# One VectorE operation for the silu of the state-space convolution, tile by tile, and both decay increments made ahead

## The chip, the cores and the metric

The program runs on one core of a Trainium2 chip. The metric is the time of one execution on the device in microseconds (us). The kernel before took 2345.67 us, the median of three runs (2345.67, 2345.67 and 2346.8).

## The reference, cut to what matters

Two layers of a decoder trunk on 512 tokens of width 1024. In each layer one input projection of the normalised residual feeds four token mixers: A (dilated attention), B (retention), C (differential attention) and D (a Mamba-2 state space). Their outputs are gated, summed and projected; then come a cross-attention over 256 memory tokens and a SwiGLU. The change lies in D:

```python
xbc = conv(xbc, conv_w, 4 taps, depthwise, causal) + conv_b     # 1024 channels
xbc = silu(xbc)                                                 # a * sigmoid(a)
xs, Bm, Cm = split(xbc, (512, 256, 256))
dt = softplus(dt + dt_bias);  a_cum = cumsum(dt * A)            # 8 heads in 2 groups
Lmat = exp(where(causal, a_cum[i] - a_cum[j], -1e30))           # decay, per head and 128-token chunk
y_diag = einsum(C B^T * Lmat, x * dt);  y_off = C h_prev * exp(a_cum)
y = rmsnorm((y_diag + y_off + x * D) * silu(z))
```

## The kernel before, in words

All activations lie feature-major in tiles of 128 features by 512 tokens ("units", 59 of them; some in "quads" of four side by side). Each large product is made of three products in fp32r, high part by high, high by low and low by high (`mm3`, `tm`), so that PE gets 128x128 weights and 512 columns for each instruction.

**The weight stream.** The weights come in chunks of eight 128x128 blocks through SP's DMA queue (`load`, L231). `prep` makes of a chunk its high part on ACT (L245) and its low part on POOL or VectorE (L248; three chunks of five go to POOL). It is called when PE's program comes to a new chunk, and makes the chunk three places further on (`PREP = 3`); four buffers hold the high parts, four the low.

**The order of the work** is written out once, by a planner in Python; no engine reorders anything. PE's program is the large products of the projections. After every three products `beat` counts 3, and at each 6 (so every six products) `step` lets every active item of a queue go on by one stage. The items are generators: what they issue up to the next `yield n` goes into all engines' programs at this place, and they go on n steps later. At most three items are active, the others wait in order. `bu` waits for free units, `bgbanks` for PSUM banks, `turn` for a count that other items raise, `finish` makes steps without large products until the named items are done.

**State space.** The 1024 channels of x, B and C are eight tiles: the first four come out of one group of products at once, the other four one by one (`ev_rb`, L418). After every second tile an item `conv` is queued for the pair: bias and last tap on ACT (L705), six multiply-adds on VectorE (L708), after three steps the tanh on ACT (L713; all weights are halved, so silu(2a) = a tanh(a) + a), after two more a product (L716) and a sum (L718) for each tile on POOL. `dt_item` makes the step sizes and the increments of the decay. Then come the products for z (`tm`, 32 blocks), and after them `d_item` is queued for each of the four chunks of 128 tokens; it starts once all of `conv` and `dt_item` is done.

A `d_item` builds the decay as exp(products): `tri_a(g)` (L795, two POOL operations for a group of four heads, high and low part) writes the increments masked by a triangle into two units, PE multiplies them with the strict triangle `stri` (L825, L826, through L266), ACT takes the exponential (L827). Both groups use the same two units, so `tri_a(1)` is issued behind group 0's products, three steps before its own. Between lie the transposes of the chunk (L803), the copies out of PSUM (L810, L811, L812), the products with dt and the decay on VectorE (L818, L819) and the skip term on POOL (L820).

```python
tri_a(0)                                    # L800
... transposes, copies; yield 3; L818 to L820; yield 3
self.mm(self.P(b), self.stri, self.UR(ta[0]), True, False)   # L825, in the loop over g
if g == 0:
    tri_a(1)                                # L830
    yield 3
```

The queues behind this: ACT holds `prep`'s high parts and `conv`'s tanh in one program; POOL holds `prep`'s low parts, L716, L718, L795 and L820 in one program.

Of the kernel before, what the change touches and what calls it, by code (L numbers as in the profile page):

```python
# [12 lines left out]
AF = mybir.ActivationFunctionType  # L13
# [44 lines left out]
class Prog:  # L58
# [18 lines left out]

# [1 line left out]
    def unit(self, n=1, r=False):  # L79
        """n tiles of [128, 512]; r: for products, of 12 significant bits"""  # L80
        if self.nu < n:
            raise RuntimeError("out of units")
        self.nu -= n
        v = self.vid
        self.vid += n
        for i in range(v, v + n):
            self.tiles[i] = self.upool.tile([128, 512], F32R if r else F32, tag="u", name="u")
        return v

    def quad(self, r=False):  # L90
        """four tiles of [128, 512] side by side"""
        if self.nq < 1:
            raise RuntimeError("out of quads")
        self.nq -= 1
        v = self.vid
        self.vid += 4
        t = self.qpool.tile([128, 4, 512], F32R if r else F32, tag="q", name="q")
        self.quads[v] = t
        for i in range(4):
            self.tiles[v + i] = t[:, i]  # L100
        return v
# [44 lines left out]
    def bu(self, n=1, r=False):  # L146
        """units for background work, once enough are free"""
        while self.nu < n + self.reserve:
            yield
        us = [self.unit(r=r) for _ in range(n)]  # L150
        return us if n > 1 else us[0]
# [8 lines left out]

# [1 line left out]
    def add(self, name, gen):  # L162
# [7 lines left out]
    def turn(self, key, n):  # L170
        """waits for the n-th turn at key"""
        while self.turns.get(key, 0) < n:
            yield
# [12 lines left out]
    def go(self, it):  # L186
        """one stage of an item; it yields how many beats its next stage should wait"""
        it[2] -= 1
        if it[2] > 0:
            return  # L190
        try:
            it[2] = next(it[1]) or 1
        except StopIteration:
            self.active.remove(it)
            self.left[it[0]] -= 1
# [29 lines left out]

# [1 line left out]
    def load(self, n):  # L227
# [46 lines left out]
    def fm(self, name, l, cols, xs, evac, outer=False, k0=0, norm=None, need=None):  # L274
        """feature-major products: one bank per 128 columns; outer: all columns of one k before the next;
        norm: the outputs wait for the norm of the products' input, which is found meanwhile"""
        K = len(xs)
        if outer:
            bs = [self.bank() for _ in cols]
            for k in range(K):  # L280
                if need:
                    need(k)
                for j, c in enumerate(cols):
                    self.mm3(self.P(bs[j]), self.w(name, l, k0 + k, c), xs[k], k == 0, k == K - 1)

            def out():
                if norm:
                    self.norm_bcast()
                    norm()
                for j, b in enumerate(bs):  # L290
                    evac(j, self.P(b))
                    self.freebank(b)
            if norm:
                self.norm_stat()
                self.later = [18, out]
            else:
                out()
            return
        for j, c in enumerate(cols):
            b = self.bank()  # L300
            for k in range(K):
                self.mm3(self.P(b), self.w(name, l, k0 + k, c), xs[k], k == 0, k == K - 1)
            evac(j, self.P(b))
            self.freebank(b)

    def tm(self, name, l, c0, xs, evac, nt=NT):
        """token-major products: 512 columns, one bank per 128 tokens"""
        K = len(xs)
# [13 lines left out]

# [1 line left out]
    def rsqrt(self, v, w):  # L324
        """1/sqrt(v) of a [128, w] tile: bit guess and three Newton steps"""
        nc = self.nc
# [14 lines left out]
    def split(self, hi, lo, src):  # L341
        """hi + lo = src, each of 12 significant bits"""
        self.nc.scalar.activation(out=hi, in_=src, func=AF.Copy)  # L343
        self.nc.vector.tensor_tensor(out=lo, in0=src, in1=hi.bitcast(F32), op=OP.subtract)
# [9 lines left out]

# [1 line left out]
    def finish_x(self, d, ps, g, hi=True):  # L356
        """the residual tile d is final: its part of the norm and of the next input"""
        nc = self.nc
# [67 lines left out]

# [1 line left out]
    def a_item(self, pr, qb):  # L428
# [57 lines left out]

# [1 line left out]
    def c_item(self, h, qb):  # L488
# [84 lines left out]
    def tail(self, name, b, g, t):  # L573
        """a transposed bank [feature, 4, token] times its gains becomes a branch's input"""
        nc = self.nc
# [12 lines left out]

# [1 line left out]
    def b_item(self, l, t):  # L590
# [103 lines left out]

# [1 line left out]
    def conv(self, l, js):  # L696
        nc = self.nc
        cw = lambda i, j: self.cw[:, j * 4 + i:j * 4 + i + 1]
        X = [self.U(self.D[1] + j) for j in js]
        yield from self.turn("conv", js[0])  # L700
        us = yield from self.bu(2 * len(js))
        A = [self.U(u) for u in us[::2]]
        th = [self.U(u) for u in us[1::2]]
        for j, x, a in zip(js, X, A):
            nc.scalar.activation(out=a, in_=x, func=AF.Identity, scale=cw(3, j), bias=self.cw[:, 32 + j:33 + j])  # L705
        for i in range(1, 4):
            for j, x, a in zip(js, X, A):
                nc.vector.scalar_tensor_tensor(out=a[:, i:], in0=x[:, :T - i], scalar=cw(3 - i, j), in1=a[:, i:],  # L708
                                               op0=OP.mult, op1=OP.add)
        yield 3  # L710
        self.turns["conv"] = js[0] + 2
        for t, a in zip(th, A):
            nc.scalar.activation(out=t, in_=a, func=AF.Tanh)  # L713
        yield 2
        for x, t, a in zip(X, th, A):
            nc.gpsimd.tensor_tensor(out=x, in0=t, in1=a, op=OP.mult)  # L716
        for x, a in zip(X, A):
            nc.gpsimd.tensor_tensor(out=x, in0=x, in1=a, op=OP.add)  # L718
        for u in us:
            self.release(u)  # L720

# [59 lines left out]
    def d_item(self, l, c):  # L781
# [8 lines left out]
        b8 = lambda ap: ap.unsqueeze(2).to_broadcast([128, 8, 64])  # L790
        ta = yield from self.bu(2, True)

        def tri_a(g):
            for u, a in zip(ta, (S["ah"], S["al"])):
                nc.gpsimd.tensor_tensor(  # L795
# [3 lines left out]
                    op=OP.mult)  # L799
        tri_a(0)  # L800
        bs = yield from self.bgbanks(2)
        for j in range(4):
# [20 lines left out]
        for g in range(2):  # L823
            (b,) = yield from self.bgbanks(1)
            self.mm(self.P(b), self.stri, self.UR(ta[0]), True, False)  # L825
            self.mm(self.P(b), self.stri, self.UR(ta[1]), False, True)  # L826
            nc.scalar.activation(out=self.U(G[g]), in_=self.P(b), func=AF.Exp)  # L827
            self.bgfree(b)
            if g == 0:
                tri_a(1)  # L830
                yield 3
        yield 1
        self.release(ta[0])
        self.release(ta[1])
        for g in range(2):
# [71 lines left out]

# [1 line left out]
    def upgate(self, l, i, name):  # L909
# [43 lines left out]

# [1 line left out]
    def mem_load(self, i):  # L955
# [135 lines left out]

# [1 line left out]
    def ffn(self, l, g, last):  # L1093
# [51 lines left out]

# [1 line left out]
    def layer(self, l):  # L1147
# [41 lines left out]
        def ev_x(o):  # L1189
            f = self.ev_rb(xb + o)  # L1190

            def g(j, ps):
                f(j, ps)
                if j % 2:
                    self.add("Dc", self.conv(l, [o + j - 1, o + j]))
            return g
# [254 lines left out]
```

## Time and profile before

| | |
|---|---|
| profiled execution, span | 2340.9 us, 27338 instructions |
| the same kernel, timed runs | 2345.67, 2346.8, 2345.67 us |
| PE busy | 2285.5 us (98%) |
| VectorE (DVE) busy | 1170.2 us (50%) |
| ScalarE (ACT) busy | 820.9 us (35%) |
| GpSimd (POOL) busy | 656.2 us (28%) |
| mean granted TensorE clock | 0.993 |

The profiled execution has no time of its own beside its span; the timed runs lie 4.8 us above the span, which is what starts and ends an execution around its first and last instruction. "Busy" is the share of the span in which an engine executes; an arrow in a row names what an idle engine waited for; PEclk is the granted clock of TensorE, 1.00 for 2.4 GHz and 0.50 for 1.2 GHz.

### The profile page before, as it was taken

What the parts mean: (1) busy time and instruction counts of PE and PEld (TensorE: products, weight loads), DVE (VectorE), ACT (ScalarE), POOL (GpSimd) and SP (SyncE); (2) the same over time, 40 slices, a digit from 0 to 9 for tenths busy, and PEclk for the clock granted to TensorE, in tenths of its full rate; (3) what the DMA queues carried; (4) which work ended last, traced back from release to release, by engine and by line L of the source; (5) the groups of instructions that cost most, each with busy time, mean ns of one, the idle gap of its engine ahead of it and who ended that gap; (6) DMA issues with size and microseconds to landing.
All of it is one profiled execution on the core that took longest, in us unless ns stands there. A gap on an engine that the chain in (4) does not pass through costs nothing. (4 is left out here: it accounts for less than half of the span.)

```text
span 2340.9 us, 27338 instructions
## 1 busy us (share of the span) xinstructions
PE 2285.5 (98%) x10714; PEld 1835.9 (78%) x10714; DVE 1170.2 (50%) x2186; ACT 820.9 (35%) x1395; POOL 656.2 (28%) x327
## 2 busy tenths in 40 slices
PE   8999999999999999999999999999999999999997
PEld 6777777777888788888877777777878877888886
DVE  6755443545846554431347563355475655543321
ACT  5323433343234432222323244334423443322231
POOL 2463222213222122222237422222322222222221
PEclk9999999999999999999999999999999999999998
DMA  6122222223234223333322222222223432332331
GB/s 227 51 81 73 78 76 73 81 72 95 78 99 144 72 90 108 99 92 107 122 88 80 67 79 73 73 81 76 92 68 99 138 105 81 90 99 90 100 98 54
DMA packets 61473, 213.70 MB, mean 91 GB/s; under 512 B 7072, under 2 KB 7456, under 8 KB 61088
## 3 DMA queue, kind: packets, MB, share of 16 engines
q1 hardware_dynamic: 60624, 210.18, 28.7%
q8 instruction: 84, 1.38, 0.2%
q10 hardware_dynamic: 576, 1.05, 0.1%
q0 software_dynamic: 144, 0.73, 0.1%
q14 instruction: 45, 0.37, 0.0%
HBM read 207.73 MB, written 4.19 MB: 91 GB/s over the span
## 5 line engine op out<-in xcount | busy, mean ns | idle before, releaser
L266 PE MATMUL ps<-u,hi 128*128 128x512 f32 x4160 | 1301.9, 394 | 1.3 <-ACT u L343 0.7
L248 POOL TENSOR_TENSOR lo<-raw,hi 128x1024 fp32r<-128x1024 f32 x213 | 519.0, 2438 | 1567.8 <-ACT hi L245 1505.3
L266 PEld LDWEIGHTS ps<-u,hi 128*128 128x128 f32 x4160 | 772.6, 188 | 173.8 <-issue 12.9
L266 PE MATMUL ps<-u,lo 128*128 128x512 f32 x2080 | 812.3, 391 | 1.7 <-POOL lo L248 1.7
L245 ACT ACTIVATE hi<-raw 128x1024 fp32r<-128x1024 f32 x372 | 388.8, 1051 | 329.9 <-PE ps L266 220.1
L266 PEld LDWEIGHTS ps<-u,lo 128*128 128x128 f32 x2080 | 391.0, 188 | 85.3 <-POOL lo L248 2.4
L248 DVE TENSOR_TENSOR lo<-raw,hi 128x1024 fp32r<-128x1024 f32 x159 | 209.5, 1320 | 352.2 <-ACT hi L245 351.9
L266 PE MATMUL ps<-hi,u 128*128 128x512 f32 x896 | 289.9, 405 | 11.6 <-ACT hi L245 11.6
L266 PE MATMUL ps<-q,hi 128*128 128x512 f32 x768 | 240.8, 395 | 0.0
L266 PEld LDWEIGHTS ps<-hi,u 128*128 128x128 f32 x896 | 166.1, 192 | 56.0 <-ACT hi L245 12.9
L266 PE MATMUL ps<-lo,u 128*128 128x512 f32 x448 | 178.2, 398 | 6.7 <-POOL lo L248 5.6
L266 PE MATMUL ps<-u 128*64 128x128 f32 (+6 forms) x1208 | 171.0, 338 | 4.3 <-DVE u L418 2.1
L266 PEld LDWEIGHTS ps<-q,hi 128*128 128x128 f32 x768 | 141.3, 188 | 34.0 <-issue 5.2
L266 PEld LDWEIGHTS ps<-u 128*128 128x128 f32 (+2 forms) x1208 | 117.1, 172 | 47.5 <-issue 27.9
L266 PE MATMUL ps<-q,lo 128*128 128x512 f32 x384 | 149.8, 390 | 0.0
L921 ACT ACTIVATE u<-u 128x512 f32<-128x512 f32 x64 | 40.4, 631 | 210.9 <-DVE u L920 210.6
L266 PEld LDWEIGHTS ps<-lo,u 128*128 128x128 f32 x448 | 85.7, 191 | 28.3 <-POOL lo L248 6.9
L920 DVE TENSOR_TENSOR u<-ps,u 128x512 f32<-128x512 f32 x64 | 44.0, 688 | 121.8 <-PE ps L266 121.8
L266 PEld LDWEIGHTS ps<-q,lo 128*128 128x128 f32 x384 | 72.1, 188 | 15.5
L1108 DVE TENSOR_TENSOR u<-ps,u 128x512 f32<-128x512 f32 x44 | 30.4, 692 | 86.7 <-PE ps L266 85.9
L347 PE MATMUL ps<-gcst,u 128*128 128x128 f32 x416 | 65.9, 274 | 5.9 <-DVE u L684 2.8
L347 PEld LDWEIGHTS ps<-gcst,u 128*128 128x128 f32 x416 | 51.2, 140 | 23.0 <-DVE u L684 4.1
(209 smaller groups left out, 1657.2 us busy)
## 6 DMA issues: line engine op xcount, KB each, us to landing
raw<-wall SPq DMA_DIRECT2D x372, 512.0 KB, 3.5
q<-memt SPq DMA_DIRECT2D x6, 512.0 KB, 6.4
q<-xt SPq DMA_DIRECT2D x2, 1024.0 KB, 7.6
u<-rot SPq DMA_DIRECT2D x8, 256.0 KB, 4.1
u<-xt SPq DMA_DIRECT2D x8, 256.0 KB, 6.0
xd<-u SPq DMA_DIRECT2D x8, 256.0 KB, 2.0
u<-xd SPq DMA_DIRECT2D x8, 256.0 KB, 5.0
out<-u SPq DMA_DIRECT2D x4, 256.0 KB, 2.7
```

The costliest lines, as they stand in the source:

```text
L245: nc.scalar.activation(out=h, in_=r, func=AF.Copy)
L248: eng.tensor_tensor(out=lo, in0=r, in1=h.bitcast(F32), op=OP.subtract)
L266: self.nc.tensor.matmul(out, lhsT=a, rhs=b, start=start, stop=stop)
L347: self.nc.tensor.transpose(out, src, self.ident)
L920: nc.vector.tensor_tensor(out=self.U(u), in0=ps, in1=self.U(self.rb), op=OP.mult)
L921: nc.scalar.activation(out=self.U(u), in_=self.U(u), func=AF.Tanh, scale=0.5)
L1108: nc.vector.tensor_tensor(out=self.U(t), in0=ps, in1=self.U(self.rb), op=OP.mult)
```

## The change

`conv` becomes an item of one tile instead of two. It issues the bias and last tap on ACT, one step later three multiply-adds on VectorE, two steps later it lets the next tile's item begin, one step later the tanh on ACT, and two steps later one VectorE operation, x = (tanh + 1) * a, instead of the two on POOL. It is queued after every tile.

`d_item` takes four units for the increments instead of two. `tri_a(0)` stands where it stood, `tri_a(1)` two steps behind it and ahead of the transposes; the transposes and what follows them up to group 0's products move two steps back; the two groups' products are one step apart instead of three, and a group's units are released right behind its products. From `tri_a(0)` to the products with the decay (L837) it is ten steps as before. Comments are removed as well.

```diff
-    def conv(self, l, js):
+    def conv(self, l, j):
...
-        yield from self.turn("conv", js[0])
-        us = yield from self.bu(2 * len(js))
...
-        for j, x, a in zip(js, X, A):
-            nc.scalar.activation(out=a, in_=x, func=AF.Identity, scale=cw(3, j), bias=self.cw[:, 32 + j:33 + j])
+        yield from self.turn("conv", j)
+        ua, ut = yield from self.bu(2)
+        a, th = self.U(ua), self.U(ut)
+        nc.scalar.activation(out=a, in_=x, func=AF.Identity, scale=cw(3), bias=self.cw[:, 32 + j:33 + j])
+        yield 1
         for i in range(1, 4):
-            for j, x, a in zip(js, X, A):
-                nc.vector.scalar_tensor_tensor(out=a[:, i:], in0=x[:, :T - i], scalar=cw(3 - i, j), in1=a[:, i:],
-                                               op0=OP.mult, op1=OP.add)
-        yield 3
-        self.turns["conv"] = js[0] + 2
-        for t, a in zip(th, A):
-            nc.scalar.activation(out=t, in_=a, func=AF.Tanh)
+            nc.vector.scalar_tensor_tensor(out=a[:, i:], in0=x[:, :T - i], scalar=cw(3 - i), in1=a[:, i:],
+                                           op0=OP.mult, op1=OP.add)
         yield 2
-        for x, t, a in zip(X, th, A):
-            nc.gpsimd.tensor_tensor(out=x, in0=t, in1=a, op=OP.mult)
-        for x, a in zip(X, A):
-            nc.gpsimd.tensor_tensor(out=x, in0=x, in1=a, op=OP.add)
-        for u in us:
-            self.release(u)
+        self.passed("conv")
+        yield 1
+        nc.scalar.activation(out=th, in_=a, func=AF.Tanh)
+        yield 2
+        nc.vector.scalar_tensor_tensor(out=x, in0=th, scalar=1.0, in1=a, op0=OP.add, op1=OP.mult)
+        self.release(ua)
+        self.release(ut)
...
-        ta = yield from self.bu(2, True)
+        ta = yield from self.bu(4, True)
 
         def tri_a(g):
-            for u, a in zip(ta, (S["ah"], S["al"])):
+            for u, a in zip(ta[2 * g:2 * g + 2], (S["ah"], S["al"])):
...
         tri_a(0)
+        yield 2
+        tri_a(1)
         bs = yield from self.bgbanks(2)
...
-            self.mm(self.P(b), self.stri, self.UR(ta[0]), True, False)
-            self.mm(self.P(b), self.stri, self.UR(ta[1]), False, True)
+            self.mm(self.P(b), self.stri, self.UR(ta[2 * g]), True, False)
+            self.mm(self.P(b), self.stri, self.UR(ta[2 * g + 1]), False, True)
+            self.release(ta[2 * g])
+            self.release(ta[2 * g + 1])
             nc.scalar.activation(out=self.U(G[g]), in_=self.P(b), func=AF.Exp)
             self.bgfree(b)
-            if g == 0:
-                tri_a(1)
-                yield 3
-        yield 1
-        self.release(ta[0])
-        self.release(ta[1])
+            yield 1
...
-                if j % 2:
-                    self.add("Dc", self.conv(l, [o + j - 1, o + j]))
+                self.add("Dc", self.conv(l, o + j))
```

## Rows read from the trace of the kernel before

**Rows 1.** The page: span, and busy time and share of each engine.
```profile
span 2340.9 us, 27338 instructions
...
PE 2285.5 (98%) x10714; PEld 1835.9 (78%) x10714; DVE 1170.2 (50%) x2186; ACT 820.9 (35%) x1395; POOL 656.2 (28%) x327
```

**Rows 2.** Waits of PE, 60 to 220 us (layer 0): us in total, times, longest.
```profile
PE ps L266 <- POOL u L795: 7.1, 4, 3.8
PE ps L266 <- POOL lo L248: 3.4, 2, 1.7
...
PE ps L266 <- ACT hi L245: 0.3, 2, 0.2
```

**Rows 3.** Waits of PE, 1200 to 1300 us (layer 1), same columns.
```profile
PE ps L266 <- POOL lo L248: 3.9, 2, 2.2
PE ps L266 <- POOL u L795: 1.9, 3, 0.8
PE ps L266 <- ACT hi L245: 1.2, 1, 1.2
```

**Rows 4.** Busy time by stretch: window, us, engines' busy us (instructions), PEclk, DMA, GB/s.
```profile
70.00:112.00 42.00, 40.12 (x181) 32.56 (x180) 38.13 (x54) 12.68 (x19) 22.64 (x13) 1.00 0.18 56
116.00:120.00 4.00, 3.92 (x10) 3.16 (x11) 1.11 (x1) 2.48 (x5) 4.00 (x4) 0.57 0.38 131
140.00:148.00 8.00, 4.42 (x12) 3.27 (x13) 4.58 (x5) 0.81 (x2) 8.00 (x8) 0.79 0.20 66
196.00:204.00 8.00, 7.14 (x24) 5.74 (x25) 0.69 (x1) 1.66 (x2) 1.49 (x2) 0.79 0.21 76
1248.00:1256.00 8.00, 7.00 (x24) 5.57 (x24) 7.82 (x5) 0.86 (x2) 8.00 (x6) 0.79 0.23 68
1256.00:1264.00 8.00, 5.82 (x19) 4.37 (x18) 5.06 (x5) 3.59 (x8) 8.00 (x5) 0.79 0.30 78
```

**Rows 5.** Timeline of ACT, layer 0: start, us, line and operation [idle before, releaser].
```profile
98.02 1.29 ACT L713 ACTIVATE u<-u 128x512 f32<-128x512 f32 x2 [9.91 <-DVE u L708]
99.22 1.99 ACT L245 ACTIVATE hi<-raw 128x1024 fp32r<-128x1024 f32 x2
```

**Rows 6.** Waits of ACT, 1205 to 1270 us.
```profile
ACT u L713 <- DVE u L708: 23.1, 4, 9.9
```

**Rows 7.** Timeline of DVE: six multiply-adds, in layer 0 and in layer 1.
```profile
94.54 4.05 DVE L708 SCALAR_TENSOR_TENSOR u<-q,cw,u 128x511 f32<-128x511 f32 x6
...
1248.18 10.82 DVE L708 SCALAR_TENSOR_TENSOR u<-q,cw,u 128x511 f32<-128x511 f32 x6 [2.16 <-ACT u L705]
```

**Rows 8.** Groups of DVE, 64 to 125 us, then 1210 to 1270 us: busy, mean ns.
```profile
L708 DVE SCALAR_TENSOR_TENSOR u<-q,cw,u 128x511 f32<-128x511 f32 (+2 forms) x24 | 23.4, 1042 | 0.0
...
L708 DVE SCALAR_TENSOR_TENSOR u<-q,cw,u 128x511 f32<-128x511 f32 (+2 forms) x24 | 28.2, 1240 | 3.0 <-ACT u L705 3.0
```

**Rows 9.** Line 880, the same operation elsewhere: ns min/median/max, first and last start.
```profile
L880 DVE SCALAR_TENSOR_TENSOR q<-u,q x8: 679/682/1834, 178.9 to 1358.0; 128x512 f32<-128x512 f32 x8
```

**Rows 10.** Groups of POOL over the whole span: busy, mean ns.
```profile
L718 POOL TENSOR_TENSOR q<-q,u 128x512 f32<-128x512 f32 x16 | 26.9, 1698 | 0.0
L716 POOL TENSOR_TENSOR q<-u 128x512 f32<-128x512 f32 x16 | 25.1, 1588 | 63.3 <-ACT u L713 63.3
```

**Rows 11.** Timeline of POOL, layer 0, around the decay increments.
```profile
126.64 1.03 POOL L795 TENSOR_TENSOR u<-gcst,d_ah 128x512 fp32r<-128x512 f32 x1
...
134.51 2.94 POOL L820 TENSOR_TENSOR u<-u,vec 128x512 f32<-128x512 f32 x2
137.42 2.82 POOL L248 TENSOR_TENSOR lo<-raw,hi 128x1024 fp32r<-128x1024 f32 x1
...
141.66 1.48 POOL L795 TENSOR_TENSOR u<-gcst,d_ah 128x512 fp32r<-128x512 f32 x1
```

**Rows 12.** Timeline of PE, layer 0: two products each of two successive groups of three.
```profile
95.91 0.61 PE L266 MATMUL ps<-hi,u 128*128 128x512 f32 x2
...
96.59 0.61 PE L266 MATMUL ps<-hi,u 128*128 128x512 f32 x2
```

More of the change, by code (lines that the diff above doesn't have):

```diff
@@ L693, in b_item @@
         yield from self.tail("B", b, self.vc(l, V_GN, 4), t)
-    def conv(self, l, js):
+    def conv(self, l, j):
         nc = self.nc
-        cw = lambda i, j: self.cw[:, j * 4 + i:j * 4 + i + 1]
-        X = [self.U(self.D[1] + j) for j in js]
-        yield from self.turn("conv", js[0])
-        us = yield from self.bu(2 * len(js))
-        A = [self.U(u) for u in us[::2]]
-        th = [self.U(u) for u in us[1::2]]
-        for j, x, a in zip(js, X, A):
-            nc.scalar.activation(out=a, in_=x, func=AF.Identity, scale=cw(3, j), bias=self.cw[:, 32 + j:33 + j])
-        for i in range(1, 4):
-            for j, x, a in zip(js, X, A):
-                nc.vector.scalar_tensor_tensor(out=a[:, i:], in0=x[:, :T - i], scalar=cw(3 - i, j), in1=a[:, i:],
-                                               op0=OP.mult, op1=OP.add)
-        yield 3
-        self.turns["conv"] = js[0] + 2
-        for t, a in zip(th, A):
-            nc.scalar.activation(out=t, in_=a, func=AF.Tanh)
-        yield 2
-        for x, t, a in zip(X, th, A):
-            nc.gpsimd.tensor_tensor(out=x, in0=t, in1=a, op=OP.mult)
-        for x, a in zip(X, A):
-            nc.gpsimd.tensor_tensor(out=x, in0=x, in1=a, op=OP.add)
-        for u in us:
-            self.release(u)
+        cw = lambda i: self.cw[:, j * 4 + i:j * 4 + i + 1]
+        x = self.U(self.D[1] + j)
+        yield from self.turn("conv", j)
[3 more added lines that the diff above has]
+        yield 1
+        for i in range(1, 4):
+            nc.vector.scalar_tensor_tensor(out=a[:, i:], in0=x[:, :T - i], scalar=cw(3 - i), in1=a[:, i:],
+                                           op0=OP.mult, op1=OP.add)
+        yield 2
+        self.passed("conv")
[5 more added lines that the diff above has]
+        self.release(ut)
     def dt_item(self, l):
```

## The prediction

> **What bounds the kernel now.** The page comes first: PE is busy for 2285.5 of 2340.9 us [rows 1], so an engine other than PE matters only where PE waits for it. The second view is therefore the waits of PE, stage by stage. In the state-space stage of layer 0 PE waits 7.1 us for the decay increments (L795), 3.4 us for the weight stream's low parts and 0.3 us for its high parts [rows 2]; in layer 1 the same three are 1.9, 3.9 and 1.2 us [rows 3]. That is 9.0 us for increments and 8.8 us for weights. The third view is the busy time by stretch, for its granted clock: each of five stretches in or behind these waits has a clock below 1.00, 0.57 over 4 us or 0.79 over 8 us [rows 4]. A product takes twice as long at 1.2 GHz as at 2.4, so a stretch loses (1 - clock) times its length: 0.43 x 4 = 1.72 us once, 0.21 x 8 = 1.68 us four times. The stretches at 116, 1248 and 1256 us lie at waits for weights (5.1 us together), those at 140 and 196 us at waits for increments (3.4 us). So
>
> - waits for weights: 8.8 + 5.1 = 13.9 us
> - waits for increments: 9.0 + 3.4 = 12.4 us
>
> The fourth view, the timelines, says why weights are late. ACT stands 9.91 us before a tanh of `conv` until VectorE's multiply-adds are done, and the two high parts right behind it in ACT's program come late by that [rows 5]; such waits are 23.1 us in layer 1 [rows 6]. VectorE is late because it is nearly full (38.1 busy of 42 us [rows 4]) and because the same six multiply-adds take 4.05 us at one place and 10.82 us at another [rows 7]. The long ones coincide with L716 and L718 on POOL, which take 1.6 to 1.7 us each, 52 us in all [rows 10]. POOL's low parts also stand behind these. The increments are late because POOL has three skip terms (2 x 1.47 and one more) and a low part of 2.82 us ahead of the second group's [rows 11].
>
> **The change, conv.** Removed: 32 operations on POOL, 52.0 us [rows 10]. Added: 16 on VectorE, of the form of L880, at 0.68 us [rows 9], so 8 x 0.68 = 5.4 us in each layer; between 0.68 and the longest L880, 1.83, they are 5.4 to 14.7 us. I take 0.68, because POOL falls silent in this stage but for its low parts. The 24 multiply-adds of a layer take 23.4 us in layer 0 and 28.2 us in layer 1 [rows 8]; at the 4.05 / 6 = 0.675 us of the undisturbed six they would take 16.2 us. What else VectorE does there is 38.1 - 23.4 = 14.7 us. Its work per layer becomes 16.2 + 5.4 + 14.7 = 36.3 us, less than the 38.1 of before although it has eight more operations.
>
> Time for it: two successive groups of three products start 0.68 us apart [rows 12], a step of the planner is six products, so 1.36 us. The new items follow each other every three steps and the last needs four more: 8 x 3 + 4 = 28 steps, 38.1 us. VectorE's 36.3 us fit, with a backlog of a few us while `dt_item`'s small operations pass. A backlog delays tanh, and with it ACT's next high part. What hides that is the stream's lead: three chunks of 24 products are 16.3 us, less 1.0 us for a high part [rows 5] and 2.8 us for a low one [rows 11], so 12.5 us. I cost conv's waits at zero after the change and take all 13.9 us. The cover is gone where the backlog passes 12.5 us; PE then waits for the excess.
>
> The convolution also ends later. Before, the last pair began 16 steps after the first (32 blocks of B and C's tiles) and ended five later; now it is 28 steps. `d_item` begins only after those 32 blocks and the 32 of z, 32 steps: four are left as cover. Beyond them the items would slip by 1.36 us a step, which costs nothing while PE has the products of A and C to do.
>
> **The change, increments.** For three items together, POOL's new order is twelve L795 first, then the skip terms. `tri_a(1)` issues two POOL operations and no DMA. On POOL it passes the skip term and whatever low part lies there; these come up to 2 x 1.48 us later for each item. The low part has the 12.5 us of above, and the skip term is first read after the decayed products, more than six steps away. PE's transposes, the copies on ACT and VectorE and the products with dt go two steps back; PE has large products in those steps, and the decayed products stay ten steps behind `tri_a(0)`. Group 0's products come two steps later, group 1's at the same place.
>
> Is twelve in front enough? Even if POOL began no earlier than now, at 126.64 us [rows 11], at 1.03 to 1.48 us each (1.26 in the middle) the six up to the first item's second group end at 134.2, the ten up to the second's at 139.2, the twelve at 141.8. PE's present wait ended after 141.66 + two operations [rows 11], 3.8 us late at the longest [rows 2], so it asks for the first from about 139.4, and for the others 1.36 and 2.7 us later: met, the last by 0.3 us. And POOL will begin earlier, since conv's operations ahead of it are gone. The fourth item has POOL nearly alone, with one low part between. I cost all waits for increments at zero, but hold 2 us back for what the margins of under 2 us may leave.
>
> More units (four instead of two) can hold an item up only where fewer than six are free; it then waits in the planner, not on an engine.
>
> **Sum.** 13.9 + 12.4 - 2 = 24.3 us. The span would be 2340.9 - 24.3 = 2316.6; the runs lie 4.8 us above their span, so 2345.67 - 24.3 = 2321.4, **2321 us**. Nothing later takes it back: PE is in order, its next waits are local, and a product not waited for is done earlier to the end.
>
> **A rule against it.** The Trainium skill, in "Advanced Engine Details and Errata", section "GPSIMD Details", says that the Pool engine shares a read and a write interface with VectorE and conflicts with VectorE's instructions that have two SBUF inputs. The multiply-adds and the new operation are such instructions, and 4.05 against 10.82 us for the same six [rows 7] agrees. By this rule 32 such operations a layer stay exposed to whatever POOL still runs; the second and the last rival below are this.
>
> **Rivals.**
>
> - *The increments stay late* (the low parts hold POOL up, or its units come free late): only conv's 13.9 us are won, 2332 us. For it: a low part needs ACT's high part first and blocks POOL's queue. Against: the order above. 10%.
> - *The tanh stays late.* If VectorE's operations keep layer 1's mean of 1.24 us [rows 8], its work is 32 x 1.24 + 14.7 = 54.4 us, the backlog 16.3, the excess over 12.5 us 3.8 us in each layer; with two slow stretches of 1.7 us that is 11 us of new waits, 26.3 - 11 = 15 won, 2330 us. Against: the long ones are beside conv's own POOL operations. 10%.
> - *It does not do what it says*: the waits move on to the next wait of the same stage (the state's sum, the exponential), because VectorE's and ACT's part of `d_item` is no faster, and what PE gains per layer it gives back there; about 2346 us. For it: this chain is long. Against: PE's waits in these stretches are nearly all of the three kinds. 7%.
> - *Slower*: VectorE becomes the bound. If each of the 32 takes the 10.82 / 6 = 1.80 us of layer 1's worst six [rows 7], its work is 57.6 + 14.7 = 72.3 us, the backlog 34.2, the excess 21.7 us a layer; 43.4 + 3.4 for the clock is 47 of new waits against 26 won, 2345.67 + 21 = 2366 us. It is slower from the point where 2 x (backlog - 12.5) + 3.4 = 26.3, a backlog of 24 us, 1.48 us per operation. Against: POOL would have to run all the time beside it. 7%.
>
> **How the numbers follow.** The forecast has 66%, with its own range of 2317 to 2326: 2319.4 if nothing is held back, less a little for changed small waits elsewhere, and up to 5 us more for new ones. The range 2316 to 2334 takes in the first two rivals and holds 86%; the others are left out. A measurement of this kernel can tell about 0.2% (4.7 us) from no change. Faster: 66 + 10 + 10 = 86%; within 0.2%: 7%; slower: 7%.
>
> **What would show it.** In the profile after: no L716 or L718; the multiply-adds at 0.7 us each and the new operation at 0.68; PE's waits for L795 and for L248's low parts in both stages under 1 us each; the granted clock 1.00 in all stretches between 40 us and the end; ACT's waits before tanh under 5 us at a time; later stages as before. Wrong for conv, if PE's waits for weights stay with ACT's tanh before them; wrong for the increments, if L795 still releases PE; wrong in the sum, if PE waits on something new in the state-space stage.

## The result, and the profile after

The changed kernel takes 2313.59 us (median; 2313.1 to 2315.54), the kernel before 2345.67 us (2344.01 to 2346.8) beside it: a ratio of 0.9869, with a 95% interval of 0.9857 to 0.9881. That is 32.1 us less, where 24.3 were forecast, and 2.4 us below the lower end of the range (2316).

The page of the changed kernel, span and busy times:

```profile
span 2313.7 us, 27318 instructions
...
PE 2274.4 (98%) x10714; PEld 1832.7 (79%) x10714; DVE 1171.7 (51%) x2202; ACT 821.1 (35%) x1395; POOL 604.4 (26%) x295
```

PE's waits in the state-space stage of layer 0, 60 to 220 us (us, times, longest), which answer to [rows 2]:

```profile
PE ps L266 <- ACT u L874: 0.8, 1, 0.8
PE ps L347 <- DVE q L894: 0.2, 1, 0.2
```

Neither increments nor weights are left in it; from 1180 to 1300 us, the place of [rows 3], no wait of PE is listed at all. The stretches that answer to [rows 4] (window, us, busy us of PE, PEld, DVE, ACT, POOL with instructions, PEclk, DMA):

```profile
70.00:112.00 42.00, 42.00 (x191) 34.73 (x190) 39.73 (x66) 16.64 (x26) 7.73 (x3) 1.00 0.24 75
115.00:123.00 8.00, 8.00 (x42) 6.75 (x41) 3.86 (x5) 4.30 (x7) 5.67 (x4) 1.00 0.47 139
134.00:146.00 12.00, 12.00 (x57) 10.06 (x56) 11.96 (x9) 4.46 (x7) 10.45 (x6) 1.00 0.19 51
185.00:197.00 12.00, 12.00 (x63) 10.25 (x62) 2.07 (x3) 2.64 (x3) 2.39 (x1) 1.00 0.33 113
1232.00:1248.00 16.00, 16.00 (x73) 13.23 (x72) 10.22 (x13) 8.61 (x14) 5.64 (x3) 1.00 0.32 98
```

PE is busy throughout and the clock is 1.00. VectorE, however, is busy for 39.7 of the first 42 us, more than the 38.1 of before. ACT's waits before the tanh in layer 0 (for [rows 5, 6]):

```profile
ACT u L713 <- DVE u L708: 17.4, 5, 6.3
```

The multiply-adds, line 708, in the whole span, and the new operation (ns min/median/max, first and last start):

```profile
L708 DVE SCALAR_TENSOR_TENSOR u<-q,cw,u x48: 739/750/2890, 72.6 to 1236.9; 128x511 f32<-128x511 f32 x16, 128x510 f32<-128x510 f32 x16, 128x509 f32<-128x509 f32 x16
...
L715 DVE SCALAR_TENSOR_TENSOR q<-u x16: 676/684/689, 79.4 to 1242.6; 128x512 f32<-128x512 f32 x16
```

POOL's program for the first three items in layer 0 (start, us), which answers to [rows 11]: a low part, then twelve operations of the increments (first and last shown), and the next low part; the skip terms come behind it.

```profile
117.33 2.40 POOL L248 TENSOR_TENSOR lo<-raw,hi 128x1024 fp32r<-128x1024 f32 x1 [5.58 <-ACT hi L245]
119.68 1.04 POOL L792 TENSOR_TENSOR u<-gcst,d_ah 128x512 fp32r<-128x512 f32 x1
...
133.00 1.48 POOL L792 TENSOR_TENSOR u<-gcst,d_al 128x512 fp32r<-128x512 f32 x1
134.45 2.84 POOL L248 TENSOR_TENSOR lo<-raw,hi 128x1024 fp32r<-128x1024 f32 x1
```

**Where the time came from.** One instruction in PE's timeline marks each layer's beginning (the sixteen products of dt), another the end (two small products of the final norm). Before, then after:

```profile
61.08 3.86 PE L266 MATMUL ps<-u,wdt 128*16 128x512 f32 x16
...
1206.17 3.86 PE L266 MATMUL ps<-u,wdt 128*16 128x512 f32 x16
...
2322.31 0.28 PE L266 MATMUL ps<-gcst,u 128*128 128x1 f32 x2
```

```profile
63.57 3.86 PE L266 MATMUL ps<-u,wdt 128*16 128x512 f32 x16
...
1190.92 3.86 PE L266 MATMUL ps<-u,wdt 128*16 128x512 f32 x16
...
2295.48 0.28 PE L266 MATMUL ps<-gcst,u 128*128 128x1 f32 x2
```

From the first to the second it is 1145.1 us before and 1127.4 after, 17.7 less; from the second to the third 1116.1 and 1104.6, 11.6 less. Together 29.3 us. Ahead of the first mark the profiled execution after is 2.5 us later; the spans differ by 27.2.

### The profile page after: what moved, and what is told of

The parts are those of the page before. It is cut to its first block, busy times and chain, and to the rows that moved or that the text cites. A ratio compares the mean times of both kernels' runs of the same rounds, so it can differ in the third digit from the quotient of the medians.

```text
span 2313.7 us, 27318 instructions
## 1 busy us (share of the span) xinstructions
PE 2274.4 (98%) x10714; PEld 1832.7 (79%) x10714; DVE 1171.7 (51%) x2202; ACT 821.1 (35%) x1395; POOL 604.4 (26%) x295
## 4 chain that ended last, share of the span: by engine, by line
PE 70%; DVE 4%; ACT 1%; issue 0%; DVEq 0%; ACTq 0%
PE ps L266 69%; PE ps L347 1%; DVE u L683 0%; DVE u L680 0%; DVE rq_a L335 0%; DVE bst L667 0%; DVE rq_a L334 0%; DVE rq_z L337 0%; DVE u L684 0%; DVE lo L248 0%; DVE u L659 0%; DVE rq_i L328 0%; DVE u L926 0%; DVE q L586 0%; DVE u L928 0%
## 5 line engine op out<-in xcount | busy, mean ns | idle before, releaser
L248 DVE TENSOR_TENSOR lo<-raw,hi 128x1024 fp32r<-128x1024 f32 x159 | 204.1, 1286 | 334.3 <-ACT hi L245 334.0
L266 PEld LDWEIGHTS ps<-hi,u 128*128 128x128 f32 x896 | 165.0, 190 | 54.4 <-ACT hi L245 11.6
```

The lines of the kernel that those rows point to most:

```text
L248: eng.tensor_tensor(out=lo, in0=r, in1=h.bitcast(F32), op=OP.subtract)
L266: self.nc.tensor.matmul(out, lhsT=a, rhs=b, start=start, stop=stop)
```

## The experiments

**One part alone.** The first kernel has the new `conv` and the old `d_item`, the second the old `conv` and the new `d_item`.

> The new convolution (tile by tile, silu as one VectorE operation), the decay increments as before. Theory: the two parts add; counted by the slots that PE's products lose (the gap between two starts less the 0.227 us of a product) and by the granted clock, the waits for weights cost 6.1 us in layer 0 and 9.0 us in layer 1, so 15 us less than before, about 2331 us, and PE's waits for L795 stay near 9 us. Rival: conv's POOL operations also held up the increments, then those waits shrink too and it wins over 20 us, 2325 us or less.

Measured: 2325.62 us, ratio 0.9915 (0.9901 to 0.9928), about 20 us won. PE's waits for increments, layer 0 and layer 1:

```profile
PE ps L266 <- POOL u L792: 5.5, 5, 2.0
...
PE ps L266 <- POOL u L792: 2.1, 3, 0.8
```

Waits for weights are gone in both stages, so that part is as both theories had it. Waits for increments fall only from 9.0 to 7.6 us, but they are split up: where [rows 2] have one of 3.8 us, three of 0.8 to 0.9 are left. The gain is at the rival's size, since one slow stretch is left of five, behind the wait at 186 us: conv's POOL operations had held up the increments too. POOL's timeline says why these stay late although POOL begins them 9.5 us earlier than in [rows 11] (117.15 against 126.64): the first group's end at 124.6, and the second group's stand behind the skip terms and a low part.

```profile
124.58 1.49 POOL L817 TENSOR_TENSOR u<-u,vec 128x512 f32<-128x512 f32 x1
...
128.21 2.84 POOL L248 TENSOR_TENSOR lo<-raw,hi 128x1024 fp32r<-128x1024 f32 x1
131.02 1.49 POOL L817 TENSOR_TENSOR u<-u,vec 128x512 f32<-128x512 f32 x1
132.47 1.03 POOL L792 TENSOR_TENSOR u<-gcst,d_ah 128x512 fp32r<-128x512 f32 x1
```

> The convolution as before (pairs, silu as two POOL operations), the increments of both groups ahead in four units. Theory: the waits for L795 go, which cost 11.4 us in layer 0 and 2.5 us in layer 1 in lost slots and clock, so about 2332 us, and the waits for weights stay near 9 us. Rival: POOL is still held up by conv's operations, the increments stay late by a few us and it wins 5 to 10 us only, 2336 to 2341 us.

Measured: 2331.22 us, ratio 0.994 (0.9927 to 0.9953), about 14.6 us won, as the theory said. No wait for increments is left; PE's waits for low parts in the two layers are

```profile
PE ps L266 <- POOL lo L248: 6.0, 3, 2.5
...
PE ps L266 <- POOL lo L248: 4.0, 2, 2.3
```

against 3.4 and 3.9 before. The third wait of layer 0 is new, and the longest. The twelve operations don't cause it: PE waits for the first of two low parts that POOL runs ahead of them, behind conv's own operations (PE's wait, then POOL's low parts and the first of the twelve).

```profile
124.84 0.50 PE L266 MATMUL ps<-u,lo 128*128 128x512 f32 x1 [2.54 <-POOL lo L248]
...
122.46 4.67 POOL L248 TENSOR_TENSOR lo<-raw,hi 128x1024 fp32r<-128x1024 f32 x2
127.10 1.03 POOL L795 TENSOR_TENSOR u<-gcst,d_ah 128x512 fp32r<-128x512 f32 x1
```

Why PE comes to it early enough to wait was not followed up. The parts alone win 20.2 and 14.6 against the 2345.83 us of before beside them; both together win 32, so the sum holds but for 2.7 us.

**The place or the units?** The second group's increments get units of their own, but stay in their old place.

```diff
-        ta = yield from self.bu(2, True)
+        ta = yield from self.bu(4, True)
...
         if g == 0:
             tri_a(1)
```

> The new convolution, four units for the increments, but the second group's increments issued where they were, behind the first group's products. If the place in POOL's program is what counts, it is as the new convolution alone: 2325 us, L795 waits of 7 to 8 us. If two more units are what counts (no wait for the first group's products), it is as the changed kernel, 2314 us.

Measured: 2326.2 us, ratio 0.9925 (0.991 to 0.994); the waits are 4.4 and 2.0 us. More units alone bring nothing; the place in the programs does it, and the units only make the place possible. The transposes and the products behind them, which the change moves as well, were not tried apart from it.

**The engine or the order?** Of the convolution's two edits, each alone, with the increments ahead in both: pairs with the silu on VectorE (first line), and tile by tile with it on POOL (the other two).

```diff
+            nc.vector.scalar_tensor_tensor(out=x, in0=t, scalar=1.0, in1=a, op0=OP.add, op1=OP.mult)
...
+        nc.gpsimd.tensor_tensor(out=x, in0=th, in1=a, op=OP.mult)
+        nc.gpsimd.tensor_tensor(out=x, in0=x, in1=a, op=OP.add)
```

> Pairs of tiles as before, but the silu as one VectorE operation for each tile, and the increments ahead. If taking the 32 operations off POOL is what helps (it frees POOL, and the multiply-adds run undisturbed), this is as fast as the changed kernel, 2313 to 2316 us. If it is the finer order of the items, the waits for weights stay and it is at 2325 to 2331 us.

> Tile by tile as changed, increments ahead, but the silu as the two POOL operations of before. If taking the work off POOL is what helps, the multiply-adds stay at 1.0 to 1.2 us and the waits for weights at several us: 2325 to 2331 us. If the finer order is what helps, 2313 to 2317 us.

Measured: 2313.57 us in pairs on VectorE (ratio 0.9861, 0.9847 to 0.9875), the changed kernel's time; 2325.68 us tile by tile on POOL (0.9916, 0.9902 to 0.993). The kernel with the increments ahead and conv as before, measured beside them, took 2331.22 us. So moving the silu off POOL wins 17.7 us in pairs and 12.1 tile by tile; going tile by tile wins 5.5 us while the silu is on POOL, and nothing once it is on VectorE. The multiply-adds in the two kernels (busy us, mean ns), pairs on VectorE first:

```profile
L708 DVE SCALAR_TENSOR_TENSOR u<-q,cw,u 128x511 f32<-128x511 f32 (+2 forms) x48 | 38.3, 866 | 0.9 <-ACT u L705 0.9
```

```profile
L708 DVE SCALAR_TENSOR_TENSOR u<-q,cw,u 128x511 f32<-128x511 f32 (+2 forms) x48 | 61.5, 1287 | 3.3 <-ACT u L705 2.2
```

PE's waits in the second are not where I had put them: its weights come in time, but the products of B with C behind the transposes wait for the last tile's silu (one line for each layer), and in layer 1 the increments are late again.

```profile
PE ps L266 <- POOL q L716: 2.7, 1, 2.7
...
PE ps L266 <- POOL u L793: 2.8, 2, 1.9
PE ps L266 <- POOL q L716: 2.3, 1, 2.3
```

So weights can be in time although the multiply-adds are slower than before (1.29 us against 1.14 over both layers). What the tiles shorten is the longest stand of ACT before a tanh: 8.2 us in layer 0 and 8.4 in layer 1 (shown: ACT's waits, 1180 to 1300 us), where pairs with the silu on POOL have 9.9.

```profile
ACT u L713 <- DVE u L708: 19.3, 4, 8.4
```

**How much cover has VectorE?** The changed kernel with one more operation for each tile, and with three (`range(3)`).

```diff
+        for _ in range(1):
+            nc.vector.scalar_tensor_tensor(out=th, in0=a, scalar=1.0, in1=a, op0=OP.add, op1=OP.mult)
         yield 2
         self.passed("conv")
```

> The changed kernel with one more VectorE operation (unused result) for each tile between the multiply-adds and the tanh, 8 in each layer, about 6 us. The prediction's cover: the backlog grows from the 6.3 us of the longest wait before a tanh to about 12, inside the 12.5 us that the stream's lead allows: 2313 to 2316 us. If VectorE was already the bound there: 12 us slower.

> The changed kernel with three more VectorE operations for each tile, 24 in each layer, 16 to 19 us. The prediction's cover: the backlog grows to about 24 us, 11 to 12 us over the lead of 12.5, so PE waits 11 us in each layer for weights, with slow stretches 2313.6 + 22 + 3 to 7 = 2339 to 2343 us. If the multiply-adds have no cover it is 2346 us or more, if the lead is longer than worked out 2320 us.

Measured: 2323.51 us with one (ratio 0.9915, 0.99 to 0.9929) and 2346.78 us with three (1.0009, 1.0 to 1.0019). The first expectation of the lighter load failed; 13.1 us of added work cost 10 us, near the second (12).

```profile
L711 DVE SCALAR_TENSOR_TENSOR u<-u 128x512 f32<-128x512 f32 x16 | 13.1, 820 | 0.6
```

Weights are still in time there, as worked out; the waits came back at the increments, in layer 0 and in layer 1:

```profile
PE ps L266 <- POOL u L794: 2.2, 3, 0.9
...
PE ps L266 <- POOL u L794: 3.9, 3, 2.0
```

POOL's timeline of layer 0 shows the way: ACT's high part is later, so is the low part in front of the twelve operations, which end at 140.2 instead of 134.5.

```profile
120.81 2.39 POOL L248 TENSOR_TENSOR lo<-raw,hi 128x1024 fp32r<-128x1024 f32 x1 [6.35 <-ACT hi L245]
...
138.72 1.49 POOL L794 TENSOR_TENSOR u<-gcst,d_al 128x512 fp32r<-128x512 f32 x1
```

With three, 35.3 us of added work cost 33 us, outside the 2339 to 2343 us expected and at the price that stood there for no cover. PE now waits for weights too (the longest: 4.2 us for a high part in layer 0, 3.5 for a low part in layer 1; 5.8 and 5.6 us in all, half of the 11 expected in each layer), for increments (1.0 and 4.6 us) and for the last silu (2.1 and 1.2 us).

```profile
PE ps L266 <- ACT hi L245: 4.2, 1, 4.2
...
PE ps L266 <- POOL u L794: 4.6, 5, 2.0
PE ps L266 <- DVE lo L248: 3.5, 1, 3.5
```

The same single operation was added to the kernel in pairs:

```diff
+        for t, a in zip(th, A):
+            nc.vector.scalar_tensor_tensor(out=t, in0=a, scalar=1.0, in1=a, op0=OP.add, op1=OP.mult)
         yield 3
```

> Pairs of tiles with the silu as one VectorE operation and the increments ahead (2313.6 us), with one more VectorE operation (unused result) for each tile ahead of the tanh, 16 in all, as in the kernel with one more operation per tile, which lost 10 us. Theory: that kernel lost because VectorE's whole work in the stage stands at its limit; two independent chains of multiply-adds go every 0.66 us where one goes every 0.78, and were disturbed less, 10 us less VectorE time over both layers, so there is room for the 11 to 13 us: 2313 to 2317 us. Rival: any added work ahead of the tanh is paid, about 2323 us.

Measured: 2318.18 us (ratio 0.9885, 0.9868 to 0.9901), 4.6 us more than in pairs without it, between the two expectations. It has no wait for increments, but one of 2.2 us for a low part in layer 1, behind a tanh that ACT stands 8.4 us for (ACT's waits, 1180 to 1300 us):

```profile
ACT u L715 <- DVE u L711: 20.7, 3, 8.4
```

So a kernel with 10 us less VectorE work in its multiply-adds bears the load better, but not for nothing. Part of the difference is the load itself, which takes 10.3 us here and 13.1 there. What share is total work and what share the place ahead of the tanh stays open.

**The kernel before, again.** Three more profiles of it, unchanged.

> The kernel before, unchanged, with another profile. The profiles so far end 1.8 us before their run's time, and the runs of the kernel before range from 2340 to 2349 us. Theory: the profiled execution on which the sum was made (span 2340.9, so about 2342.7 us) was a short one; a typical one has a span of about 2344 us, with 2 to 4 us more of the same waits (L795, L248) and slow stretches. Rival: the span is 2341 again and the runs have 4.8 us around it.

> The kernel before, unchanged: a third profile, to catch one of its longer executions (up to 2349 us). Theory: what a longer one has more is waits of PE and slow stretches in the two state-space stages (40 to 220 and 1180 to 1345 us), nothing elsewhere. Rival: it is longer in the start, before 40 us.

> The kernel before, unchanged: a fourth profile, with the same theory and rival as the third.

Measured: the first has a span of 2338.9 us at 2340.74 us; all ten runs of it lie 1.7 to 1.9 us above their spans, which go from 2338.9 to 2345.9 (median time 2345.23). So there is no 4.8 us around a span, and the execution on which the prediction's sum was made was a short one. The other two are long ones, 2347.65 us (span 2345.8) and 2348.58 us (span 2346.8). The third has the waits of [rows 2, 3] to the tenth; it is slower at the start, from 35 to 43 us:

```profile
35.00:43.00 8.00, 6.74 (x21) 5.27 (x21) 7.09 (x9) 8.00 (x13) 0.00 (x0) 0.59 0.52 141
```

In the profile of the prediction the clock is 1.00 there; 0.41 x 8 = 3.3 us of the 4.9 by which it is longer. That is the rival. The fourth has a stretch at the start as well, and slower clocks behind the same waits for increments, and one in the retention stage:

```profile
35.00:43.00 8.00, 7.75 (x31) 6.28 (x32) 7.81 (x11) 8.00 (x14) 0.00 (x0) 0.79 0.67 201
142.00:154.00 12.00, 8.09 (x23) 6.10 (x24) 7.66 (x6) 1.96 (x4) 11.89 (x9) 0.72 0.15 44
196.00:208.00 12.00, 9.10 (x27) 6.77 (x26) 4.18 (x3) 1.61 (x2) 4.39 (x3) 0.72 0.27 88
1764.00:1772.00 8.00, 7.38 (x32) 5.84 (x33) 7.06 (x9) 2.10 (x3) 2.39 (x1) 0.79 0.44 132
```

In the profile of the prediction the second and third have 0.86. So the two longer executions differ from the one of the prediction less in their waits (by about 1 us at most) than in how long the clock is low behind them. The theory that a longer one has more waits fell; of the four places where the fourth's clock is lower, two lie in a state-space stage and two elsewhere, and behind the wait at 116 us [rows 4] its clock did not fall.

## Why the prediction was wrong

The direction held, and the two kinds of wait went as forecast; the size did not hold: 32.1 us where 24.3 were forecast. The step that failed is the **Sum**, in three terms.

1. *PE's waits were taken from the view of waits* (9.0 + 8.8 us, with 8.4 for the clock: 26.3). The marks say 29.3. That view counts idle time only from the modelled end of the product before, 0.39 us after its start, while without a wait the next would have started after 0.23 us; and the product after a wait holds PE longer too (0.50 us instead of 0.39, first line). The timeline of the kernel before, at a wait for a low part and at its longest wait:

```profile
102.76 0.50 PE L266 MATMUL ps<-lo,u 128*128 128x512 f32 x1 [1.71 <-POOL lo L248]
...
139.02 0.39 PE L266 MATMUL ps<-u,lo 128*128 128x512 f32 x1
143.20 0.62 PE L266 MATMUL ps<-u,stri 128*128 128x512 f32 x1 [3.79 <-POOL u L795]
144.20 0.80 PE L266 MATMUL ps<-u,stri 128*128 128x512 f32 x1 [0.38 <-POOL u L795]
```

   At the longest, idle 3.79 and 0.38 us; but from start to start it is 4.18 and 1.00 us, of which 0.23 each would have been needed: 3.95 and 0.77 us lost (the second partly to the slow clock of [rows 4], which must not be counted twice). Over 14 such waits this makes about 3 us. The expectations of the two parts, which count by starts and by the clock, come to 15.1 us for weights and 13.9 for increments, together 29.0.
2. *2 us were held back* for margins; nothing was left in these stages but waits of 0.8 and 0.2 us, of neither kind.
3. *"4.8 us above the span" compared a span with the runs of other executions.* It is 1.8 us; the profiled execution before would have shown about 2342.7 us, 3.0 below the median. So a usual execution before had 3.0 us more to lose than the sum was made on. The later profiles show such differences in the clock, but not which of them the change takes away. The profiled one after, with 2315.54, is 1.9 above its own median, mostly by the 2.5 us of its start.

Together 3.0 + 2.0 + 3.0 - 0.2 (the small rest: start, end and the run after) = 7.8 us, the difference.

By its other steps:

- *Waits for weights from ACT behind the tanh*: right; conv alone removes them. *POOL as the disturber*: right for the multiply-adds' time, in part for the weights. With the silu on POOL tile by tile, multiply-adds of 1.29 us no longer make weights late; the 12 us that this kernel loses are other waits, for the last silu and for increments.
- *13.9 us for weights, 12.4 for increments*: the split did not hold. Conv alone won 20.2 us (17.9 between the spans of the two profiles), not the 13.9 of the first rival, in part because its POOL operations also held up the increments.
- *The increments wait for their place in POOL's program*: right, and the two units are only the means. The twelve operations begin at 119.7 us and end at 134.5, ahead of the 141.8 worked out.
- *The multiply-adds fall to 0.675 us*: wrong. They take 0.75 us, tile by tile 2.31 us for three, and those beside a low part on POOL up to 2.89: 48.3 us in all instead of the 32.4 forecast, against 51.6 before. VectorE's work did not shrink, 39.7 of 42 us, so the weights are not in time for the reason given there; that they are was partly luck. ACT now stands at most 6.3 us before a tanh, where it stood 9.9.
- *The convolution's waits cost nothing up to a backlog of 12.5 us*: true of the weights in the changed kernel and with one more operation, but 12.5 us is not their cover: in the pairs with load a stand of 8.4 us before a tanh made a low part 2.2 us late, as stands of 9.9 did in the kernel before. For PE it is wrong. The longest wait before a tanh is 6.3 us, not under 5, and 6 us more in each layer cost 5: the high part that ACT holds back stands in POOL's program ahead of the increments, whose margin is smaller. By this load the changed kernel lies near the edge of its cover.
- *Slower from a backlog of 24 us*, that is 62 us of VectorE work in a layer: the load of three brings it to 24.1 + 5.5 + 17.6 + 14.7 = 62 us, and it is at the time of before (ratio 1.0009). The point agrees, the price does not: 33 us were lost where the rival had 26.3, and only 11.4 us of it are waits for weights; four slow stretches, at 1.7 to 3.4 us, and the waits for increments and the silu make up most of the rest.

## What to carry to other kernels

Price a stall of a pipelined engine from start to start, less the slot that an undisturbed instruction takes, and add the slow clock behind it once; the idle time in a view of waits is a lower bound. When two edits are tried alone, compare all four combinations: an edit that adds nothing to another can still win by itself. Before a profile's span is set against a median, look at how far runs of that kernel scatter, and at their own spans. A second group's work that waits in an in-order queue gains by its place, and a cover worked out for one consumer of a queue doesn't hold for the next that stands behind it there.

## What the runs showed of the hardware that was not expected

A multiply-add of VectorE takes 0.75 us alone. In pairs, six in 4.05 us, the next begins before the last has ended; three that each need the one before go in 2.31 us, one every 0.78 us. Beside a low part on POOL three take 4.34 us instead of 2.31, 2.0 us more for a low part of 2.55 (last line).

```profile
86.42 2.31 DVE L708 SCALAR_TENSOR_TENSOR u<-q,cw,u 128x511 f32<-128x511 f32 x3
...
89.25 4.34 DVE L708 SCALAR_TENSOR_TENSOR u<-q,cw,u 128x511 f32<-128x511 f32 x3
...
90.49 2.55 POOL L248 TENSOR_TENSOR lo<-raw,hi 128x1024 fp32r<-128x1024 f32 x1 [69.80 <-ACT hi L245]
```

The Trainium skill's rule of a shared interface ("Advanced Engine Details and Errata", section "GPSIMD Details") agrees with the direction; how long an operation of 0.75 us then takes, up to 2.89 us, is this trace's. And the clock of TensorE differs between executions of one kernel: 0.86 or 0.72 over the same 12 us behind the same wait for increments (3.8 us at the longest in both).
